# A hybrid encoder block: y in tiles of token halves, and two units' first products ahead of the second half's sums

## The chip, the cores and the metric

One core of a Trainium2 chip runs the whole program in one launch. The number that counts is the device time of one execution in microseconds (us). The engines are named as in the profile: PE is TensorE's matrix multiplication and PEld its weight load, DVE is VectorE, ACT is ScalarE, POOL is GpSimd, SP is SyncE, which only issues DMAs. Each engine runs its own instructions strictly in the order in which the program holds them; semaphores hold an instruction back until what it reads is there and what it overwrites is free.

## What is computed

A bidirectional encoder block over 1024 tokens of width 1024, in float32. Cut to what matters here:

```python
y = sigmoid(ga) * (h_a @ p_a) + sigmoid(gb) * (h_b @ p_b)
x = x + y @ w_o
xn = rmsnorm(x, norm2)
u = xn @ w_up                       # 1024 x 5632
u = conv3_over_tokens(u) + conv_b   # per channel
a, g = split(u, 2)
x = x + (gelu(g) * a) @ w_down
```

Each float32 matrix product is made of three products of halves: an operand is split into a high part h (rounded to the matrix engine's float32 format) and a low part l = value - h, and h*h, h*l and l*h are summed.

## The kernel before

The program is written in a framework that allocates tiles from pools with a fixed number of buffers, and whose scheduler fixes the order of each engine's instructions ahead of time from its own estimates. So the order of the code is a hint, and the order in the program is what the chip follows.

The change lies between two long stretches. Ahead of it is the product with w_o: y has its channels on partitions, in 8 high and 8 low tiles over all 1024 tokens (`yh`, `yl`). `wo_piece(w, cg, b0)` makes 256 columns of two blocks of 128 tokens with 48 matmuls and adds them to the residual `acc` (L956), the x1 tiles. The last two column groups are done for token blocks 0 to 3 first, then `norm0` normalises these blocks, then the column groups are done for blocks 4 to 7.

Behind it is the up projection in the class `Up`. It works in 22 units j of 128 a-columns and 128 g-columns, and each unit uses Strassen's scheme in Winograd's form on 2 by 2 blocks: 7 products instead of 8. The four blocks of the activations are two token halves by two halves of the channels: 11 and 12 are the first token half, 21 and 22 the second. Besides 11, 12 and 22 the products need four sums, S1 to S4, each over both token halves. A block or sum has four k-pieces kk of 128 channels by 512 tokens, each as a high and a low part (`block`, the tiles A.. and AS..). One product is 12 matmuls: 4 pieces, 3 split products. `first(u)` makes products 11 and 12, which need the first token half alone; `rest(u)` makes S2, S1, S3, S4 and 22.

`rows(half)` makes the norm of four token blocks: it stores x1 to DRAM (L1019, on GpSimd's queue), sums squares on ACT (L1021), takes the power -1/2 on GpSimd (L224) and scales the rows (L1024, `nxs`). `turn` transposes four 128 by 128 pieces on PE into one PSUM tile (L1030). `norm0` brings blocks 11 and 12 out of PSUM: the high part on ACT (L1044), a full copy f on DVE (L1045), the low part on GpSimd (L1046). `norm1` does the same for the second half (L1064 to L1067) and makes the sums on DVE (L1072 to L1075); the eight pieces' low parts are shared by DVE and GpSimd (L81).

`prep(u)` makes a unit's weights: four pairs of blocks, the high parts `uh` by ACT casts (L80) and the low parts `ul` by GpSimd (L81), and the weight sums on DVE (L1123 to L1130). The tiles whi and wlo have 4 buffers each, shared by the w_o weights and the units' weights. In `run`, the first unit's weights are loaded and made only when the w_o stage has been left.

Of the kernel before, what the change touches and what calls it, by code (L numbers as in the profile page):

```python
# [877 lines left out]
def merge_ffn(K, ha_d, hb_d, out):  # L878
    nc, tc, I = K.nc, K.tc, K.I
    V, G, A, T = nc.vector, nc.gpsimd, nc.scalar, nc.tensor  # L880
    with tc.tile_pool(name="mf", bufs=1, reuse_waits="tile") as fp, ExitStack() as es:
# [25 lines left out]
        for gidx, (hx, pname) in enumerate(((K.ha, "p_a"), (hb, "p_b"))):  # L907
            if gidx == 1:
                while len(hb[0]) < KT:
                    load_hb()  # L910
                y = h2("y", "A")
            for cg in range(4):
# [3 lines left out]
                for cb in range(2):  # L916
# [5 lines left out]
                    for half in range(2):  # L922
                        t = slice(half * 512, half * 512 + 512)
                        ps = K.small()
                        K.proj_cm(ps, w, cb * P, hx, half)
                        if gidx == 0:
                            if len(hb[0]) < KT:
                                load_hb()
                            V.scalar_tensor_tensor(ya[m][:, t], tg[:, t], 1.0, ps, op0=ALU.add, op1=ALU.mult)
                        else:  # L930
                            V.scalar_tensor_tensor(tg[:, t], tg[:, t], 1.0, ps, op0=ALU.add, op1=ALU.mult)
                            V.tensor_tensor(tg[:, t], tg[:, t], ya[m][:, t], op=ALU.add)
                            K.split(y[0][m][:, t], y[1][m][:, t], tg[:, t])
# [16 lines left out]
        def wo_piece(w, cg, b0):  # L950
            ps = K.small()
            for j in range(2):
                K.proj_tm(ps[:, j * 256:(j + 1) * 256], w, y, b0 + j)
# [12 lines left out]
        up = Up(K, g4, acc, g2, fp)  # L966
        for i in range(2):
# [12 lines left out]
class Up:  # L980
# [31 lines left out]
    def rows(self, half, scr):  # L1012
# [3 lines left out]
        for b4 in range(4):  # L1016
            blk = half * 4 + b4
            x, o = self.acc[blk], scr[b4]
            nc.gpsimd.dma_start(self.x1_d[blk * P:(blk + 1) * P, :], x)  # L1019
# [4 lines left out]
            nc.vector.tensor_scalar(o, x, r, None, op0=ALU.mult)  # L1024
# [7 lines left out]
    def norm0(self, scr, psf):  # L1032
# [16 lines left out]
    def norm1(self):  # L1049
        K, nc, G, V = self.K, self.K.nc, self.K.nc.gpsimd, self.K.nc.vector  # L1050
        xs = self.rows(1, [self.g4("nxs") for _ in range(4)])
        f2s = []

        def turns(kk):
            f2 = self.g4("f2", tag="wk")
            f2s.append(f2)
            for i in range(2):
                k = kk + 4 * i
                ps = K.small()
                self.turn(xs, k, ps)  # L1060
                t = slice(i * 512, i * 512 + 512)
                if i == 1:
                    self.b22 = self.block("22", kk, "A" if kk < 2 else "B")
                    nc.scalar.activation(self.b22[0], ps, AF.Copy, scale=self.g2[:, k:k + 1])  # L1064
                V.tensor_scalar(f2[:, t], ps, self.g2[:, k:k + 1], None, op0=ALU.mult)
                if i == 1:
                    V.tensor_tensor(self.b22[1], f2[:, t], self.b22[0].bitcast(F32), op=ALU.subtract)  # L1067

        def sums(kk):
            f, f2 = self.f[kk], f2s[kk]  # L1070
            a11, a12, a21, a22 = f[:, :512], f[:, 512:], f2[:, :512], f2[:, 512:]
            V.tensor_tensor(a22, a21, a22, op=ALU.add)  # L1072
            V.tensor_tensor(a21, a11, a21, op=ALU.subtract)
            V.tensor_tensor(a11, a22, a11, op=ALU.subtract)
            V.tensor_tensor(a12, a12, a11, op=ALU.subtract)  # L1075
            for n, (name, v) in enumerate((("S2", a11), ("S1", a22), ("S3", a21), ("S4", a12))):
                h, l = self.block(name, kk, "B" if kk >= 2 and n == 0 else "A")
                K.split(h, l, v, G if n % 2 else V)

        turns(0)  # L1080
        sums(0)
        turns(1)
        sums(1)
        turns(2)
        turns(3)
        sums(2)
        sums(3)

# [18 lines left out]
    def prep(self, u):  # L1107

        K, V, G = self.K, self.K.nc.vector, self.K.nc.gpsimd

        def pair(*blocks):
            h = K.wp.tile([P, 1024], F32R, tag="whi", bufs=NH, name=K.nm("uh"))
            l = K.wp.tile([P, 1024], F32R, tag="wlo", bufs=NW, name=K.nm("ul"))
            for n, v in enumerate(blocks):
                t = slice(n * 512, n * 512 + 512)
                K.split(h[:, t].rearrange("p (k c) -> p k c", k=4), l[:, t].rearrange("p (k c) -> p k c", k=4), v, G)
# [3 lines left out]
        yield  # L1120
# [4 lines left out]
        V.tensor_tensor(t2, u["b22"], u["b12"], op=ALU.subtract)  # L1125
        pair(t2, u["b12"])
# [16 lines left out]
    def first(self, u):  # L1143
# [4 lines left out]
        u["s"] = self.g4("s", tag="wk")  # L1148
        u["ua"], u["ug"] = self.g4("u", tag="acc"), self.g4("u", tag="acc")
        A.copy(u["s"][:, :512], u["X"])  # L1150
        self.product(u, 1, Y, True, True)
        V.tensor_tensor(u["ua"][:, :512], Y, u["s"][:, :512], op=ALU.add)

    def rest(self, u, nxt):
# [4 lines left out]
        A.copy(u["s"][:, 512:], X)  # L1159
        self.product(u, 3, Z, True, True)  # L1160
        z = self.g4("z", tag="wk")
# [5 lines left out]
        V.tensor_tensor(u["ug"][:, :512], Z, u["s"][:, 512:], op=ALU.add)  # L1167
# [20 lines left out]

    def run(self):
        us, ps = [self.load(0), self.load(1)], []  # L1190
        ps = [self.prep(u) for u in us]
        next(ps[0])
        self.first(us[0])
        self.norm1()
        next(ps[0]), next(ps[0]), next(ps[0])
        for j in range(NFF):
            u = us[j]
            if j:
                self.first(u)
            if j + 1 < NFF:  # L1200
# [112 lines left out]
```

## Time and profile before

| | us |
|---|---|
| median of 3 runs | 2235.78 (2235.41 to 2236.54) |
| the profiled execution | 2236.34 |
| its span, first to last instruction | 2234.6 |
| PE busy in it | 2136.8 (96%) |
| mean granted PE clock | 0.986 of full speed |

The span is 1.7 us shorter than the execution's own time, which also holds what lies around the first and the last instruction. PE is busy for 96% of the span, but that is an average: the stage of this change is only some 75 us long, and there PE is busy for three quarters of the time. A stretch can be read by windows (busy time of each engine between two moments), by waits (who waited for whom) and by the timeline of one engine.

### The profile page before, as it was taken

The page shows a single profiled execution, that of the slowest core. Times are in us where ns is not written, and L with a number is a line of the kernel's source. Part 1 is how long each engine was busy: PE and PEld are TensorE (multiplying, and loading weights), DVE is VectorE, ACT ScalarE, POOL GpSimd, SP SyncE. Part 2 cuts the span into 40 slices and gives each one's busy share as a digit, 9 for nine tenths or more (in the row PEclk, how much of TensorE's full clock was granted, in tenths as well). Part 3 has the DMA queues.
Part 4 walks back from the last instruction along what each step waited for, and adds up shares of the span by engine and source line. Part 5 has one row for each costly group of instructions (what it writes and reads, how often), then busy time and mean ns, then how long its engine had stood idle before and what let it go on. Part 6 is the DMA issues. An engine that isn't in the chain of part 4 may idle for free.

```text
span 2234.6 us, 30400 instructions
## 1 busy us (share of the span) xinstructions
PE 2136.8 (96%) x11936; PEld 1834.9 (82%) x11936; DVE 1303.3 (58%) x1986; ACT 912.0 (41%) x1659; POOL 680.5 (30%) x529
## 2 busy tenths in 40 slices
PE   7999999989999899999999999996999999999999
PEld 6778878888899789889888878995777877788887
DVE  4455253446597787878956334338677667673422
ACT  4333132235456556556545122124544544452221
POOL 0131101143252442533500010026666666640000
PEclk9999999999999999999999999997999999999999
DMA  3123212132211222112223574222222222295501
GB/s 124 38 82 104 66 57 76 53 71 60 57 34 50 58 40 47 57 38 62 56 90 117 160 170 147 71 86 66 76 76 85 76 68 83 85 346 193 176 29 38
DMA packets 185168, 193.85 MB, mean 87 GB/s; under 512 B 38616, under 2 KB 153336, under 8 KB 185024
## 3 DMA queue, kind: packets, MB, share of 16 engines
q1 hardware_dynamic: 175296, 156.96, 24.5%
q0 software_dynamic: 9728, 34.94, 4.4%
q8 instruction: 94, 1.54, 0.3%
q14 instruction: 50, 0.41, 0.1%
HBM read 144.38 MB, written 39.09 MB: 82 GB/s over the span
## 4 chain that ended last, share of the span: by engine, by line
PE 70%; DVE 13%; DMA 6%; issue 4%; ACT 4%; POOL 2%; SPq 0%; DVEq 0%; ACTq 0%; POOLq 0%
PE sm L105 11%; PE sm L106 11%; PE sm L107 11%; PE pj L105 8%; PE pj L106 7%; PE pj L107 7%; DMA wraw<-in_w_in_dram 3%; PE big L681 3%; PE pt L713 2%; DVE smx L685 2%; DVE p L693 1%; PE cr L465 1%; PE cr L470 1%; PE cr L467 1%; PE po L106 1%
## 5 line engine op out<-in xcount | busy, mean ns | idle before, releaser
L107 PE MATMUL pj<-whi,xn 128*128 128x256 f32 x960 | 274.1, 286 | 0.0
L105 PE MATMUL pj<-whi,xn 128*128 128x256 f32 x960 | 273.3, 285 | 0.2
L106 PE MATMUL pj<-wlo,xn 128*128 128x256 f32 x960 | 273.4, 285 | 0.0
L105 PE MATMUL pj<-xn,whi 128*128 128x512 f32 x512 | 211.9, 416 | 6.0 <-ACT xn L246 3.3
L106 PE MATMUL pj<-xn,whi 128*128 128x512 f32 x512 | 208.4, 407 | 0.0
L107 PE MATMUL pj<-xn,wlo 128*128 128x512 f32 x512 | 208.3, 407 | 0.0
L687 ACT ACTIVATE p<-big,smx 128x1024 f32<-128x1024 f32 x128 | 143.0, 1119 | 123.8 <-DVE smx L685 87.2
L81 POOL TENSOR_TENSOR ul<-ur,uh 128x512 fp32r<-128x512 f32 x110 | 173.3, 1592 | 38.4 <-ACT uh L80 38.4
L105 PEld LDWEIGHTS pj<-whi,xn 128*128 128x128 f32 x960 | 181.9, 189 | 3.2 <-ACT kT L300 0.3
L106 PEld LDWEIGHTS pj<-wlo,xn 128*128 128x128 f32 x960 | 181.8, 189 | 1.9
L107 PEld LDWEIGHTS pj<-whi,xn 128*128 128x128 f32 x960 | 181.7, 189 | 1.0
L80 ACT CAST whi<-wraw 128x1024 fp32r<-128x1024 f32 x88 | 92.2, 1048 | 216.5 <-DMA wraw<-in_w_in_dram 103.1
L685 DVE TENSOR_REDUCE smx<-big 128x1 f32<-128x1024 f32 x128 | 154.5, 1218 | 36.8 <-PE big L681 36.0
L81 DVE TENSOR_TENSOR wlo<-wraw,whi 128x1024 fp32r<-128x1024 f32 x54 | 67.6, 1251 | 168.3 <-ACT whi L80 168.3
L105 PE MATMUL sm<-AS,uh 128*128 128x512 f32 x352 | 140.5, 401 | 15.9 <-ACT AS L80 11.0
L681 PE MATMUL big<-kst,qst 128*128 128x512 f32 x512 | 146.6, 406 | 4.8 <-DMA kst<-kst 4.8
L106 PE MATMUL sm<-AS,uh 128*128 128x512 f32 x352 | 141.3, 401 | 0.6 <-POOL AS L81 0.6
L107 PE MATMUL sm<-AS,ul 128*128 128x512 f32 x352 | 140.7, 401 | 0.0
L106 PE MATMUL sm<-dl,hh 128*128 128x512 f32 x352 | 139.5, 396 | 0.0
L105 PE MATMUL sm<-dh,hh 128*128 128x512 f32 x352 | 139.0, 396 | 0.0
L107 PE MATMUL sm<-dh,hl 128*128 128x512 f32 x352 | 138.9, 396 | 0.0
L224 POOL TENSOR_TENSOR inv<-inv,mhalf 128x2 f32<-128x2 f32 x32 | 23.0, 718 | 366.9 <-DVE inv L223 308.5
(289 smaller groups left out, 5450.7 us busy)
## 6 DMA issues: line engine op xcount, KB each, us to landing
ur<-in_w_up_dram SPq DMA_DIRECT2D x88, 256.0 KB, 3.4
wr<-in_w_down_dram SPq DMA_DIRECT2D x44, 512.0 KB, 5.6
wraw<-in_w_in_dram SPq DMA_DIRECT2D x40, 512.0 KB, 5.5
wraw<-in_w_in_dram SPq DMA_DIRECT2D x48, 256.0 KB, 4.6
h_d<-cv POOLq DMA_DIRECT2D x22, 512.0 KB, 3.0
hr<-h_d SPq DMA_DIRECT2D x22, 512.0 KB, 6.5
x<-in_x_dram SPq DMA_DIRECT2D x16, 512.0 KB, 4.9
sig<-tg SPq DMA_DIRECT2D x32, 256.0 KB, 2.1
```

The costliest lines, as they stand in the source:

```text
L80: self.nc.scalar.copy(hi, src)
L81: (lo_eng or self.nc.vector).tensor_tensor(lo, src, hi.bitcast(F32), op=ALU.subtract)
L105: mm(ps, a[0], b[0], start=start, stop=False, skip_group_check=again)
L106: mm(ps, a[0], b[1], start=False, stop=False, skip_group_check=again)
L107: mm(ps, a[1], b[0], start=False, stop=stop, skip_group_check=again)
L224: K.nc.gpsimd.tensor_tensor(out, scr, K.mhalf[:scr.shape[0], :width], op=ALU.pow)
L465: T.matmul(nps[:, :MV + 1], pm[:, t], va[:, j, :], start=True, stop=i == 0)
L467: T.matmul(nps[:, :MV + 1], qs[:, t], C, start=False, stop=True)
L681: T.matmul(sps[c_][:, half * 512:half * 512 + 512], o.q[st.qp][:, c_, t], o.k[half][:, c_, s_, :], start=s_ == 0, stop=s_ == 1)
L685: V.tensor_reduce(sm[:, c_:c_ + 1], sp, op=ALU.max, axis=AX.X, negate=True)
L687: K.mark = A.activation(p_, sp, AF.Exp, bias=sm[:, c_:c_ + 1], accum_out=sm[:, 2 + c_:3 + c_]).ins
L713: T.transpose(pt[:, kk * 256 + j * P:kk * 256 + (j + 1) * P], st.w[j][:, kb * P:(kb + 1) * P], K.ident)
```

## The change

The y tiles become [token half][pair of k], so that the first half's tiles are free when the first half's w_o products are done; the blocks 11 and 12 go into them, and the copies f into the x1 buffers of the first half. The loads of units 0 and 1 are issued before the last w_o products, and `ahead()` makes the first pair of both units' weights there. `run` is now: the second half's `rows`, `first` of unit 0, all transposes (`norm1b`), `first` of unit 1, and then the sums (`norm1c`), ordered by name instead of by piece. The x1 stores move from GpSimd's queue to SP's. GpSimd no longer makes low parts of blocks and sums, nor those of unit 0's weights; DVE does these straight from PSUM where it can, and the f copies go to ACT.

```diff
-                y = h2("y", "A")
+                yt = [[[g4("y", F32R) for _ in range(KT // 2)] for _ in range(2)] for _ in range(2)]
+                y = [[[yt[p][half][k // 2][:, k % 2 * 512:k % 2 * 512 + 512] for half in range(2)]
+                      for k in range(KT)] for p in range(2)]
...
         up = Up(K, g4, acc, g2, fp)
+        up.us = [up.load(0), up.load(1)]
...
             for bp in range(2):
                 wo_piece(ws[i], 2 + i, 4 + bp * 2)
+        up.ahead()
         es.close()
...
-            nc.gpsimd.dma_start(self.x1_d[blk * P:(blk + 1) * P, :], x)
+            nc.sync.dma_start(self.x1_d[blk * P:(blk + 1) * P, :], x)
...
-            nc.vector.tensor_scalar(o, x, r, None, op0=ALU.mult)
+            if half == 1 and b4 % 2 == 0:
+                nc.scalar.activation(o, x, AF.Copy, scale=r)
+            else:
+                nc.vector.tensor_scalar(o, x, r, None, op0=ALU.mult)
...
-            f = self.g4("f", tag="B")
+            f = self.g4("f", tag="acc")
...
-                h, l = self.block(name, kk, "B")
+                h, l = self.block(name, kk, "A")
-                nc.scalar.activation(h, ps, AF.Copy, scale=self.g2[:, k:k + 1])
-                V.tensor_scalar(f[:, t], ps, self.g2[:, k:k + 1], None, op0=ALU.mult)
-                G.tensor_tensor(l, f[:, t], h.bitcast(F32), op=ALU.subtract)
+                nc.scalar.activation(h, ps, AF.Copy, scale=gk)
+                V.scalar_tensor_tensor(l, ps, gk, h.bitcast(F32), op0=ALU.mult, op1=ALU.subtract)
+                nc.scalar.activation(f[:, t], ps, AF.Copy, scale=gk)
...
+    def norm1b(self):
+        for kk in range(4):
...
+            self.turn(self.xs1, kk, ps)
+            nc.scalar.activation(v, ps, AF.Copy, scale=self.g2[:, kk:kk + 1])
...
+            self.turn(self.xs1, kk + 4, ps)
+            self.p22.append(ps)
+    def norm1c(self):
...
+            V.scalar_tensor_tensor(v, self.p22[kk], gk, a21, op0=ALU.mult, op1=ALU.add)
+            V.tensor_tensor(a21, f[:, :512], a21, op=ALU.subtract)
+            V.tensor_tensor(f[:, :512], v, f[:, :512], op=ALU.subtract)
+            K.split(*self.block("S2", kk, "A"), f[:, :512])
+            S1.append(v)
+        for kk in range(4):
+            K.split(*self.block("S1", kk, "A"), S1[kk])
+        for kk in range(4):
+            gk = self.g2[:, 4 + kk:5 + kk]
+            h, l = self.block("22", kk, "B")
+            nc.scalar.activation(h, self.p22[kk], AF.Copy, scale=gk)
+            V.scalar_tensor_tensor(l, self.p22[kk], gk, h.bitcast(F32), op0=ALU.mult, op1=ALU.subtract)
+        for kk in range(4):
+            K.split(*self.block("S3", kk, "B"), self.f2[kk])
+        for kk in range(4):
+            f = self.f[kk]
+            V.tensor_tensor(f[:, 512:], f[:, 512:], f[:, :512], op=ALU.subtract)
+            K.split(*self.block("S4", kk, "B"), f[:, 512:])
...
+        lo = V if early else G
...
+    def ahead(self):
+        self.ps = [self.prep(u, True) for u in self.us[:1]] + [self.prep(self.us[1])]
+        for p in self.ps:
+            next(p)
...
-        next(ps[0])
-        self.first(us[0])
-        self.norm1()
+        us, ps = self.us, self.ps
+        self.norm1a()
+        s = self.g4("s", tag="B")
+        self.first(us[0], s[:, :512])
+        self.norm1b()
+        self.first(us[1], s[:, 512:])
+        self.norm1c()
```

What this makes of the order of instructions shows at three places. On PE, first, where the second half's transposes end; before the change, sums come next (AS tiles, `sm` are PSUM tiles, `uh` and `ul` unit 0's weights):

```order
L1030 MATMUL sm_14430<-ident,nxs_14310 128x128
L1030 MATMUL sm_14430<-ident,nxs_14311 128x128
L1030 MATMUL sm_14430<-ident,nxs_14312 128x128
L1030 MATMUL sm_14430<-ident,nxs_14313 128x128
L105 MATMUL sm_14279<-AS_2116_14363,uh_14474 128x512
L105 MATMUL sm_14503<-AS_2118_14367,uh_14474 128x512
L106 MATMUL sm_14279<-AS_2117_14364,uh_14474 128x512
```

The same place on PE in the changed kernel, where the transposes (L1039 there) are followed by product 11 of unit 1:

```order
L1039 MATMUL sm_14393<-ident,nxs_14289 128x128
L1039 MATMUL sm_14393<-ident,nxs_14290 128x128
L1039 MATMUL sm_14393<-ident,nxs_14291 128x128
L1039 MATMUL sm_14393<-ident,nxs_14292 128x128
L105 MATMUL sm_14398<-A_2073_13999,uh_14279 128x512
L106 MATMUL sm_14398<-A_2074_14000,uh_14279 128x512
L107 MATMUL sm_14398<-A_2073_13999,ul_14280 128x512
```

So 24 matmuls that need nothing of the second half have moved between the transposes and the first sum. On DVE, second, where the second half's sums begin; before (f are full copies, A block 22's low part, AS low parts of sums):

```order
L1065 TENSOR_SCALAR f_2111_14342<-sm_14343,g_13279 128x512
L1125 TENSOR_TENSOR ut_14531<-ur_14270,ur_14267 128x512
L1065 TENSOR_SCALAR f_2111_14342<-sm_14349,g_13279 128x512
L1067 TENSOR_TENSOR A_2115_14355<-f_2111_14342,A_2114_14354 128x512
L1072 TENSOR_TENSOR f_2111_14342<-f_2111_14342 128x512
L1130 TENSOR_TENSOR ur_14270<-ur_14270,ut_14531 128x4x128
L1073 TENSOR_TENSOR f_2111_14342<-f_13981,f_2111_14342 128x512
L1074 TENSOR_TENSOR f_13981<-f_2111_14342,f_13981 128x512
L1075 TENSOR_TENSOR f_13981<-f_13981 128x512
L81 TENSOR_TENSOR AS_2117_14364<-f_13981,AS_2116_14363 128x512
```

The same place on DVE in the changed kernel (S is sum S1, f_2114 and f_2119 hold block 21):

```order
L1087 SCALAR_TENSOR_TENSOR S_2128_14428<-sm_14359,g_13279,f_2114_14352 128x512
L1088 TENSOR_TENSOR f_2114_14352<-f_13993,f_2114_14352 128x512
L1087 SCALAR_TENSOR_TENSOR S_2128_14428<-sm_14370,g_13279,f_2114_14352 128x512
L1089 TENSOR_TENSOR f_13993<-S_2128_14428,f_13993 128x512
L1087 SCALAR_TENSOR_TENSOR S_2131_14441<-sm_14382,g_13279,f_2119_14375 128x512
L1088 TENSOR_TENSOR f_2114_14352<-f_14013,f_2114_14352 128x512
L1098 SCALAR_TENSOR_TENSOR A_2139_14467<-sm_14359,g_13279,A_2138_14466 128x512
L1103 TENSOR_TENSOR f_13993<-f_13993 128x512
```

The sums of the four pieces are now made first and the low parts follow, and no preparation of weights stands between them. On GpSimd, third, from the second half's last two powers on; before:

```order
L224 TENSOR_TENSOR nr_14338<-nss_14336,mhalf 128x1
L81 TENSOR_TENSOR ul_14475<-ur_14261,uh_14474 128x512
L81 TENSOR_TENSOR ul_14475<-ut_14470,uh_14474 128x512
L81 TENSOR_TENSOR ul_14481<-ut_14470,uh_14480 128x512
L81 TENSOR_TENSOR ul_14481<-ur_14264,uh_14480 128x512
L81 TENSOR_TENSOR ul_14488<-ur_14264,uh_14487 128x512
L81 TENSOR_TENSOR ul_14492<-ur_14267,uh_14491 128x512
L81 TENSOR_TENSOR ul_14492<-ur_14270,uh_14491 128x512
L81 TENSOR_TENSOR AS_2119_14368<-f_2111_14342,AS_2118_14367 128x512
L81 TENSOR_TENSOR AS_2123_14376<-f_13981,AS_2122_14375 128x512
```

GpSimd in the changed kernel at the same place (ul_14562 and on are unit 1's low parts, ul_14618 unit 2's):

```order
L224 TENSOR_TENSOR nr_14317<-nss_14315,mhalf 128x1
L81 TENSOR_TENSOR ul_14562<-ut_14557,uh_14561 128x512
L81 TENSOR_TENSOR ul_14562<-ur_13751,uh_14561 128x512
L81 TENSOR_TENSOR ul_14594<-ut_14557,uh_14593 128x512
L81 TENSOR_TENSOR ul_14594<-ur_13754,uh_14593 128x512
L81 TENSOR_TENSOR ul_14614<-ur_13754,uh_14613 128x512
L81 TENSOR_TENSOR ul_14618<-ur_14523,uh_14617 128x512
```

Only unit 1's weights are left on GpSimd while the sums are made.

## Rows read from the trace of the kernel before

**Rows 1.** The page, part 1: busy us (share of the span) xinstructions
```profile
PE 2136.8 (96%) x11936; PEld 1834.9 (82%) x11936; DVE 1303.3 (58%) x1986; ACT 912.0 (41%) x1659; POOL 680.5 (30%) x529
```
**Rows 2.** Windows: us, busy us (instructions) of each engine, clock, DMA
```profile
1412.00:1507.90 95.90, 95.86 (x806) 95.39 (x804) 29.12 (x58) 17.15 (x26) 16.46 (x19) 1.00 0.23 78
1507.90:1582.35 74.45, 56.02 (x212) 41.86 (x213) 61.48 (x68) 34.77 (x57) 46.54 (x34) 0.84 0.21 64
```
**Rows 3.** Waits of PE, 1507.8 to 1582.4: us, times, longest us
```profile
PE sm L105 <- ACT AS L80: 11.0, 4, 5.0
PE sm L1030 <- DVE u L1152: 2.5, 1, 2.5
PE sm L105 <- ACT uh L80: 2.3, 1, 2.3
```
**Rows 4.** Timeline of PE: start us, us, line, tile, count
```profile
1507.26 0.60 PE L1030 MATMUL big<-ident,nxs 128*128 128x128 f32 x4
...
1512.63 0.63 PE L105 MATMUL sm<-A,uh 128*128 128x512 f32 x1
...
1516.89 0.63 PE L106 MATMUL sm<-A,uh 128*128 128x512 f32 x1
1517.32 1.99 PE L1030 MATMUL sm<-ident,nxs 128*128 128x128 f32 x14
...
1577.21 0.40 PE L107 MATMUL sm<-A,ul 128*128 128x512 f32 x1
...
1582.35 0.39 PE L105 MATMUL sm<-AS,uh 128*128 128x512 f32 x1
```
**Rows 5.** Timeline of DVE, the same stretch
```profile
1507.46 0.76 DVE L956 SCALAR_TENSOR_TENSOR x<-sm,x 128x256 f32<-128x256 f32 x2 [0.21 <-PE sm L107]
...
1525.11 0.74 DVE L1065 TENSOR_SCALAR f<-sm,g 128x512 f32<-128x512 f32 x1
...
1538.35 1.82 DVE L1074 TENSOR_TENSOR f<-f,f 128x512 f32<-128x512 f32 x1
...
1549.01 0.68 DVE L81 TENSOR_TENSOR AS<-f,AS 128x512 fp32r<-128x512 f32 x1
1549.61 0.68 DVE L1075 TENSOR_TENSOR f<-f 128x512 f32<-128x512 f32 x1
...
1557.35 0.68 DVE L81 TENSOR_TENSOR AS<-f,AS 128x512 fp32r<-128x512 f32 x1
```
**Rows 6.** Timeline of GpSimd, the same stretch
```profile
1506.63 1.25 POOL L224 TENSOR_TENSOR nr<-nss,mhalf 128x1 f32<-128x1 f32 x2
...
1538.32 1.30 POOL L81 TENSOR_TENSOR AS<-f,AS 128x512 fp32r<-128x512 f32 x1 [2.60 <-ACT AS L80]
...
1559.61 1.30 POOL L81 TENSOR_TENSOR ul<-ut,uh 128x512 fp32r<-128x512 f32 x1 [0.17 <-ACT uh L80]
```
**Rows 7.** Timeline of ACT, the same stretch
```profile
1489.13 1.27 ACT L1044 ACTIVATE A<-big,g 128x512 fp32r<-128x512 f32 x2 [4.77 <-PE big L1030]
...
1508.48 1.05 ACT L1021 ACTIVATE nxs<-x 128x1024 f32<-128x1024 f32 x1
...
1531.55 2.18 ACT L80 CAST AS<-f 128x512 fp32r<-128x512 f32 x4 [3.62 <-DVE f L1074]
...
1565.80 1.24 ACT L1176 ACTIVATE cv<-u,cb,cw 128x1024 f32<-128x1024 f32 x1
```
**Rows 8.** Instructions of line 247: duration ns min/median/max, first and last start
```profile
L247 DVE SCALAR_TENSOR_TENSOR xn<-cr,g,xn x16: 741/745/752, 18.2 to 50.2; 128x512 fp32r<-128x512 f32 x16
```
**Rows 9.** Timelines of GpSimd, DVE and PE in a later unit
```profile
1785.10 5.03 POOL L81 TENSOR_TENSOR ul<-ur,uh 128x512 fp32r<-128x512 f32 x4
...
1785.17 5.51 DVE L1123 TENSOR_TENSOR ut<-ur,ur 128x512 f32<-128x512 f32 x1 [3.60 <-POOL ul L81]
...
1796.74 0.51 PE L105 MATMUL sm<-AS,uh 128*128 128x512 f32 x1 [3.12 <-ACT s L1159]
```
**Rows 10.** Transfers issued by line 1019 (the x1 stores): us to landing
```profile
DMA to landing us min/median/max: 3.0/4.4/6.4
```

More of the change, by code (lines that the diff above doesn't have):

```diff
@@ L952, in wo_piece @@
             for j in range(2):
-                K.proj_tm(ps[:, j * 256:(j + 1) * 256], w, y, b0 + j)
+                half, b = divmod(b0 + j, 4)
+                K.proj_tm(ps[:, j * 256:(j + 1) * 256], w, [[t_[half] for t_ in p_] for p_ in y], b)
             for j in range(2):
@@ L1047, in norm0 @@
+                V.scalar_tensor_tensor(l, ps, gk, h.bitcast(F32), op0=ALU.mult, op1=ALU.subtract)
+                nc.scalar.activation(f[:, t], ps, AF.Copy, scale=gk)
             self.f.append(f)
[L1049 to L1087, printed above, removed]
@@ new lines, in norm1a @@
+    def norm1a(self):
+        self.xs1 = self.rows(1, [self.g4("nxs", tag="B") for _ in range(4)])
+    def norm1b(self):
+        K, nc = self.K, self.K.nc
+        self.f2, self.p22 = [], []
+        for kk in range(4):
+            if kk % 2 == 0:
+                f2 = self.g4("f2", tag="wk")
+            ps = K.small()
+            self.turn(self.xs1, kk, ps)
+            v = f2[:, kk % 2 * 512:kk % 2 * 512 + 512]
+            nc.scalar.activation(v, ps, AF.Copy, scale=self.g2[:, kk:kk + 1])
+            self.f2.append(v)
+            ps = K.small()
+            self.turn(self.xs1, kk + 4, ps)
+            self.p22.append(ps)
@@ new lines, in norm1c @@
+    def norm1c(self):
+        K, nc, V = self.K, self.K.nc, self.K.nc.vector
+        S1 = []
+        for kk in range(4):
+            if kk % 2 == 0:
+                s1 = self.g4("S1", tag="B")
+            f, a21 = self.f[kk], self.f2[kk]
+            v = s1[:, kk % 2 * 512:kk % 2 * 512 + 512]
+            gk = self.g2[:, 4 + kk:5 + kk]
[7 more added lines that the diff above has]
+        for kk in range(4):
+            gk = self.g2[:, 4 + kk:5 + kk]
+            h, l = self.block("22", kk, "B")
[3 more added lines that the diff above has]
+            K.split(*self.block("S3", kk, "B"), self.f2[kk])
+        for kk in range(4):
+            f = self.f[kk]
+            V.tensor_tensor(f[:, 512:], f[:, 512:], f[:, :512], op=ALU.subtract)
+            K.split(*self.block("S4", kk, "B"), f[:, 512:])
@@ L1105, in load, with prep @@
         return u
-    def prep(self, u):
+    def prep(self, u, early=False):
         K, V, G = self.K, self.K.nc.vector, self.K.nc.gpsimd
+        lo = V if early else G
         def pair(*blocks):
@@ L1115, in pair @@
                 t = slice(n * 512, n * 512 + 512)
-                K.split(h[:, t].rearrange("p (k c) -> p k c", k=4), l[:, t].rearrange("p (k c) -> p k c", k=4), v, G)
+                K.split(h[:, t].rearrange("p (k c) -> p k c", k=4), l[:, t].rearrange("p (k c) -> p k c", k=4), v, lo)
             u["w"].append((h, l))
         pair(u["b11"], u["b21"])
-        yield
+        if not early:
+            yield
         t = K.wp.tile([P, 1024], F32, tag="wraw", bufs=NR, name=K.nm("ut"))
@@ L1125, in prep @@
         V.tensor_tensor(t2, u["b22"], u["b12"], op=ALU.subtract)
+        if early:
+            yield
         pair(t2, u["b12"])
@@ L1147, in first @@
         self.product(u, 0, u["X"], True, True)
-        u["s"] = self.g4("s", tag="wk")
+        if s is None:
+            u["s"] = self.g4("s", tag="wk")
+            s = u["s"][:, :512]
         u["ua"], u["ug"] = self.g4("u", tag="acc"), self.g4("u", tag="acc")
-        A.copy(u["s"][:, :512], u["X"])
+        A.copy(s, u["X"])
         self.product(u, 1, Y, True, True)
-        V.tensor_tensor(u["ua"][:, :512], Y, u["s"][:, :512], op=ALU.add)
+        V.tensor_tensor(u["ua"][:, :512], Y, s, op=ALU.add)
     def rest(self, u, nxt):
@@ L1158, in rest @@
         self.product(u, 2, X, False, True)
-        A.copy(u["s"][:, 512:], X)
+        z = self.g4("z", tag="wk")
+        s2 = u["s"][:, 512:] if "s" in u else z[:, 512:]
+        A.copy(s2, X)
         self.product(u, 3, Z, True, True)
-        z = self.g4("z", tag="wk")
         A.copy(z[:, :512], Z)
@@ L1166, in rest @@
         self.product(u, 5, Z, False, True)
-        V.tensor_tensor(u["ug"][:, :512], Z, u["s"][:, 512:], op=ALU.add)
+        V.tensor_tensor(u["ug"][:, :512], Z, s2, op=ALU.add)
         step()
```

11 lines of the change are left out of this document (5 added, 6 removed).

## The prediction

> **What bounds the kernel now.** The page comes first: PE is busy for 96% of the span, DVE for 58% [rows 1], so a gain can only come from a stage in which PE waits. The windows show where the change lies in this. In the w_o stage PE is busy for 95.86 of 95.90 us; from its last transposes to the middle of unit 2 it is busy for 56.02 of 74.45 us, at a mean granted clock of 0.84 [rows 2]. The waits of that stretch name whom PE waits for: 11.0 us for the casts of the sums, 2.5 for transposes held by DVE, 2.3 for the first unit's weights [rows 3].
>
> How much is lost there? The stretch begins when the last four transposes of `norm0` end, at 1507.9, and I end it at 1582.35, where unit 2's products 11 and 12 are done [rows 4]. Its PE work is the same before and after, 180 matmuls and 32 transposes. At full clock a matmul of 512 columns takes 0.234 us (22 steps from 1577.21 to 1582.35 [rows 4]); at the lower level of 1.2 GHz, after PE had waited, 0.426 (10 steps from 1512.63 to 1516.89 [rows 4]). A transpose takes 0.14 (14 in 1.99 us [rows 4]). So the work needs 42.0 + 4.5 = 46.5 us of the 74.45: **28.0 us are lost**, 18.4 as waits (74.45 - 56.02) and the rest at the lower clock. That is all that this change can win; behind it PE's order is the same until the last unit.
>
> Behind the waits for the casts stands DVE. From the first L1065 at 1525.1 to the last low part's end at 1558.0 [rows 5] it runs 38 instructions, 0.87 us each. Two of them back to back take 0.60 (1549.01 to 1549.61 [rows 5]); one that meets GpSimd takes 1.82 instead of about 0.7 (L1074 at 1538.35, beside GpSimd's low part from 1538.32 [rows 5, 6]).
>
> **The change part by part.** I go along PE's order after the change, from the same start at 1507.9.
>
> *Ahead of it.* The y tiles hold the same numbers and cost the same splits. The early loads are issued while w_o runs; x1's stores land 3.0 to 6.4 us after their issue [rows 10], and the first f that takes an x1 buffer comes behind the first high parts, two w_o pieces (11.4 us) after that buffer's last sum: both are hidden. ACT gets eight more copies (two take 1.27 [rows 7]) and four casts of weights in the last 14 us of w_o. Before PE can transpose the third and fourth k-pairs, the PSUM tiles of the first two must be emptied: four casts (2.18 [rows 7]), the high parts and copies (0.6 each) and DVE's queue of low parts come to 5.7 us after the whi tiles come free, an estimate, and PE has 43 w_o matmuls of 0.119 us (806 instructions in 95.9 us [rows 2]) and 8 transposes there, 6.2 us. I take 0; if GpSimd's two low parts there (1.3 each [rows 6]) hold DVE longer, 2 us.
>
> *First products of unit 0.* The weights are made, so the wait of 2.3 and its low part's go, and PE stays at full clock: 24 x 0.234 = 5.6 us, to 1513.5.
>
> *Transposes.* They now need all four blocks. The last w_o result is added by 1508.2 [rows 5]; ACT is busy with casts and copies until about 1510.2, then squares two blocks (1.05 each [rows 7]), GpSimd takes the powers (0.6 each [rows 6]), and ACT scales (as long as a square, 1.05): with 0.7 for handing over, an estimate, 1514.7. PE waits **1.2 us**. Then 32 transposes, 4.5 us, to 1519.2.
>
> *First products of unit 1.* 5.6 us, to 1524.8. They cover the first sums; this is where 24 matmuls stood behind sums before.
>
> *Sums.* DVE can begin at the second transposed tile, about 1516.6. Until the last low part of S2 its order has 35 instructions. Nine read PSUM; no row here has this form in this stage, the nearest is 0.745 [rows 8], and I take 0.67 to 0.745. The others take 0.60 to 0.72. At 0.68 the 35 end at 1540.4. GpSimd keeps two low parts of unit 1 back to back in this time, 2 x 1.3 us [rows 6]. One later row shows what that can do: a DVE sum of 0.68 us took 5.51 while GpSimd ran four low parts, 5.03 us, and got in only behind the last [rows 9]. So I add the whole 2.6 us: 1543.0. The Trainium skill (SBUF — State Buffer, section "SBUF: two separate sides") says that the two engines hold the shared port pair for one whole instruction and the other blocks; by it DVE would wait behind one low part and the sum would be 1.3 us smaller. The row of 5.51 does not agree with that, and I go by the row. PE, at the lower clock after its waits, is some matmuls behind (4 for the last piece, up to 12 more): S2 and S1 of both units are done at **1545**. Between 1524.8 and there PE does 48 matmuls, 11.2 us, so it loses 9.0. Bounds: 1541, when all DVE instructions take 0.60 and meet nothing; 1550, when they average 0.87 as before and PE runs its backlog at 0.426.
>
> *Behind the sums.* Unit 0's X must be copied out before S3, and ACT has that of unit 1 behind a cast that waits for a weight tile: **0.9 us**. Then S4, S3 of both and 22 of unit 0 are 60 matmuls. Unit 2's first weights need the whi tile that 22 of unit 0 reads last: a cast (0.6) and a GpSimd low part (1.3) behind it, less three matmuls: **1.5 us**. Both units' convolutions come late together (ACT 1.24 each [rows 7]), and the copy of unit 2's X stands behind them: **1.0 us**, between 0 and 4.
>
> *The sum.* Lost after: 1.2 + 9.0 + 0.9 + 1.5 + 1.0 = 13.6 us, where 28.0 were lost before. The profiled execution took 2236.3, so 2236.3 - 14.4 = 2221.9. It is 0.6 us above the median of the runs shown, 2235.8; by the median the sum is 2221.4. I say **2222**. At the end of the up stage the order moves a little, but no wait of PE stood there that I cost.
>
> **Rivals.**
>
> *The sums stay the bound.* For it: 37 DVE instructions make the second half after, 38 before, and the stall of 5.51 shows that few meetings suffice. Against it: eight low parts of GpSimd and two sets of weight sums are gone from between them. At 0.87 each, S2's last low part comes at 1516.6 + 30.5 = 1547.1, and PE ends S1 at about 1551: 6 us of the gain go, **2228**.
>
> *No change.* The 14.4 us are spent whole: to the loss of the case above, 4 us of late convolutions and 4 us at the lower clock over the first products of unit 1 would be added. **2236**, and nothing in the rows makes all of it likely.
>
> *The sums are quick.* S1 and S2 end at 1541 and the three small waits are covered: 1.2 + 5.0 lost, **2214**.
>
> *Slower, by the w_o stage.* PE has no idle time there now [rows 2], so every wait put into it counts in full. The transposes of the third and fourth k-pairs wait for PSUM tiles that ACT now empties with twice the copies, in a row with casts that wait for w_o's own weight tiles. I found 5.7 us of work against 6.2 of cover. It decides from 14.4 us of such waits on; if ACT's and DVE's chain took three times as long, 17 us against 6.2 in two places, that is 22 us, **2243**. Against it: ACT is busy for 17 of 96 us there [rows 2], and the three durations in the chain are rows of this case.
>
> **How the numbers follow.** The forecast 0.64; sums the bound 0.14; quick 0.09; no change 0.07; slower 0.06. What a measurement can tell from no change is 0.2%, 4.5 us. The first three are faster by more than that but for a small part of the second: faster 0.86, same 0.08, slower 0.06. The range holds the bounds of the sums and the small waits and reaches to the case of 2228 and to that of 2214: 2213 to 2231, with some 0.85 inside.
>
> **What would show it.** Right: PE goes on at 1508 without a wait and at full clock into unit 0's product 11; the transposes follow within 2 us; the only long waits of PE are for casts or low parts of S2 and S1, between 1525 and 1545, about 9 us; unit 2's first low part costs 1 to 2 us; the same stretch of 180 matmuls and 32 transposes takes about 60 us. Wrong: waits of PE on PSUM tiles inside w_o; DVE sums of over 1.6 us in a row in that time, without GpSimd beside them; PE at the lower clock until S4; or waits in later units that were not there.

## The result, and the profile after

The changed kernel takes 2221.0 us, median of 4 runs, where the kernel before took 2236.2 beside it: ratio 0.9931, 95% interval 0.9919 to 0.9944. The forecast was 2222. The profiled execution took 2222.2 us, its span 2220.2, 14.4 us less than before. Two executions in the experiments, 7281 us with y's tiles alone and 2902 us with the squares behind, lie far outside all others and are left out of the ratios.

The page, part 1, as in [rows 1], and two windows, as in [rows 2]: the w_o stage, and the stretch from its last transposes to the end of unit 2's products 11 and 12 (columns: us, busy us and instructions of PE, PEld, DVE, ACT, POOL, clock, DMA share, GB/s).

```profile
PE 2132.0 (96%) x11936; PEld 1832.6 (83%) x11936; DVE 1293.1 (58%) x1991; ACT 921.5 (42%) x1673; POOL 638.9 (29%) x498
...
1412.00:1508.15 96.15, 96.15 (x808) 95.81 (x807) 34.17 (x64) 24.87 (x38) 6.32 (x8) 1.00 0.25 82
1508.15:1566.53 58.38, 50.59 (x216) 39.58 (x215) 44.96 (x65) 35.65 (x59) 17.03 (x13) 0.91 0.20 63
```

PE is still busy all through the w_o stage. The stretch that took 74.45 us takes 58.4. GpSimd was busy for 46.5 us in it and is now for 17.

The waits of PE between 1400 and 1600 us (us in total, times, longest), as in [rows 3]:

```profile
PE sm L105 <- ACT AS L80: 3.6, 1, 3.6
PE sm L105 <- ACT f L1056: 2.0, 1, 2.0
PE sm L106 <- DVE AS L81: 1.4, 1, 1.4
PE sm L107 <- POOL ul L81: 0.7, 1, 0.7
PE sm L105 <- ACT s L1185: 0.3, 1, 0.3
```

The casts of the sums cost 3.6 us instead of 11.0. The second line was not foreseen. The timeline of PE shows each at its place, as in [rows 4]:

```profile
1507.80 0.60 PE L1039 MATMUL big<-ident,nxs 128*128 128x128 f32 x4
1508.15 0.48 PE L105 MATMUL sm<-A,uh 128*128 128x512 f32 x1
...
1513.24 0.79 PE L105 MATMUL sm<-A,uh 128*128 128x512 f32 x1 [2.05 <-ACT f L1056]
1513.83 0.63 PE L106 MATMUL sm<-A,uh 128*128 128x512 f32 x1
1514.26 0.63 PE L107 MATMUL sm<-A,ul 128*128 128x512 f32 x1
...
1517.64 3.66 PE L1039 MATMUL sm<-ident,nxs 128*128 128x128 f32 x32
1521.05 0.48 PE L105 MATMUL sm<-A,uh 128*128 128x512 f32 x1
...
1526.74 0.39 PE L105 MATMUL sm<-AS,uh 128*128 128x512 f32 x1
...
1528.80 0.50 PE L107 MATMUL sm<-AS,ul 128*128 128x512 f32 x1 [0.67 <-POOL ul L81]
...
1533.40 1.05 PE L105 MATMUL sm<-AS,uh 128*128 128x512 f32 x2 [3.63 <-ACT AS L80]
1535.89 0.80 PE L106 MATMUL sm<-AS,uh 128*128 128x512 f32 x1 [1.45 <-DVE AS L81]
...
1546.93 0.39 PE L105 MATMUL sm<-AS,uh 128*128 128x512 f32 x1
...
1566.53 0.39 PE L105 MATMUL sm<-AS,uh 128*128 128x512 f32 x1
```

PE runs from the last transposes into unit 0's product 11 without a wait. Then product 12 waits 2.05 us, and seven matmuls behind it go at the lower clock (start to start 0.43 instead of 0.234; the granted clock is 0.50 of full speed from 1513.24 to 1516.39, in the window below). Unit 1's first products end at 1526.7, S2 and S1 of both units at 1546.9. From there to 1566.53 PE does 84 matmuls in 19.6 us, 0.233 each: nothing is lost there.

What product 12 waits for is the last line of this timeline of ACT:

```profile
1510.42 1.07 ACT L1027 ACTIVATE nxs<-x 128x1024 f32<-128x1024 f32 x1
...
1511.46 1.06 ACT L1027 ACTIVATE nxs<-x 128x1024 f32<-128x1024 f32 x1
...
1512.50 0.69 ACT L1056 ACTIVATE f<-big,g 128x512 f32<-128x512 f32 x1
```

f is not an input of product 12. The copy of f reads `norm0`'s last PSUM tile. That product 12's result goes where this tile was is read from the kernel, which gives up the PSUM tiles of `norm0` and makes eight new ones between the two; the trace shows that the copy ends at 1513.19 and the product starts at 1513.24. The copy stands behind two squares of the second half. The clock behind the wait, in a window as above:

```profile
1513.24:1516.39 3.15, 3.15 (x7) 2.48 (x8) 1.98 (x3) 1.62 (x2) 1.04 (x2) 0.50 0.00 0
```

In the sums, DVE meets GpSimd once; rows of DVE and of GpSimd in the same time:

```profile
1528.05 2.92 DVE L81 TENSOR_TENSOR AS<-f,AS 128x512 fp32r<-128x512 f32 x2
...
1534.56 1.28 DVE L81 TENSOR_TENSOR AS<-f,AS 128x512 fp32r<-128x512 f32 x2
...
1541.78 1.89 DVE L81 TENSOR_TENSOR AS<-f,AS 128x512 fp32r<-128x512 f32 x3
...
1527.46 1.29 POOL L81 TENSOR_TENSOR ul<-ut,uh 128x512 fp32r<-128x512 f32 x1 [13.18 <-ACT uh L80]
1528.70 1.73 POOL L81 TENSOR_TENSOR ul<-ur,uh 128x512 fp32r<-128x512 f32 x1
```

Two of DVE's instructions take 2.92 us there and 1.28 elsewhere in the sums (1534.56), so the meeting costs 1.64. In the later units the waits are those of before, shifted: the one of 3.12 us in [rows 9] comes 15.2 us earlier. One short wait is new, where the up stage ends:

```profile
1781.50 0.50 PE L105 MATMUL sm<-AS,uh 128*128 128x512 f32 x1 [3.12 <-ACT s L1185]
...
1966.46 0.50 PE L105 MATMUL sm<-AS,uh 128*128 128x512 f32 x1 [0.54 <-ACT z L1187]
```

### The profile page after: what moved, and what is told of

The parts are those of the page before. It is cut to its first block, busy times and chain, and to the rows that moved or that the text cites. A ratio compares the mean times of both kernels' runs of the same rounds, so it can differ in the third digit from the quotient of the medians.

```text
span 2220.2 us, 30362 instructions
## 1 busy us (share of the span) xinstructions
PE 2132.0 (96%) x11936; PEld 1832.6 (83%) x11936; DVE 1293.1 (58%) x1991; ACT 921.5 (42%) x1673; POOL 638.9 (29%) x498
## 4 chain that ended last, share of the span: by engine, by line
PE 68%; DVE 13%; DMA 6%; issue 5%; ACT 4%; POOL 2%; SPq 0%; ACTq 0%; DVEq 0%; POOLq 0%
PE sm L105 11%; PE sm L106 11%; PE sm L107 11%; PE pj L105 8%; PE pj L106 7%; PE pj L107 7%; PE big L681 3%; DMA wraw<-in_w_in_dram 3%; PE pt L713 2%; DVE smx L685 2%; DVE p L693 1%; PE cr L465 1%; PE cr L470 1%; PE cr L467 1%; PE po L106 1%
## 5 line engine op out<-in xcount | busy, mean ns | idle before, releaser
L81 POOL TENSOR_TENSOR ul<-ur,uh 128x512 fp32r<-128x512 f32 x105 | 165.2, 1590 | 41.8 <-ACT uh L80 41.8
```

Of the source, the lines that this page charges most:

```text
L81: (lo_eng or self.nc.vector).tensor_tensor(lo, src, hi.bitcast(F32), op=ALU.subtract)
```

## The experiments

The part of the program ahead of this stage ends at another time in each profile (product 11 of unit 0 starts between 1501.6 and 1509.8 us in kernels whose work up to there hardly differs), so the totals carry some us of chance. The table therefore has, beside the ratio, times counted in the timeline of PE from the end of w_o's last instruction, where product 11 could start: to the start of the 128th instruction (in most kernels the last of 24 + 24 matmuls of first products, 32 transposes and 48 matmuls of S2 and S1) and to the start of the 260th. At full speed the 260 need 56.6 us: 228 matmuls of 0.233, and 32 transposes of 0.107 (1517.64 to 1521.05 above).

| kernel | ratio to before (95%) | to the 128th | to the 260th |
|---|---|---|---|
| changed, the profile above | 0.9931 (0.9919 to 0.9944) | 38.5 | 69.3 |
| changed, again | 0.9925 (0.9911 to 0.9938) | 37.0 | 67.8 |
| before with y's tiles alone | 0.9997 (0.9987 to 1.0006) | | |
| casts moved in the code | 0.9921 (0.9907 to 0.9936) | 36.9 | 67.7 |
| loads late | 0.9995 (0.9986 to 1.0004) | 49.8 | 80.7 |
| loads late, stores on GpSimd | 1.0020 (1.0010 to 1.0030) | 53.7 | 84.5 |
| stores on GpSimd | 0.9926 (0.9914 to 0.9939) | 37.1 | 67.9 |
| unit 1 behind | 0.9960 (0.9945 to 0.9974) | 43.5 | 74.3 |
| low parts on GpSimd | 0.9945 (0.9929 to 0.9962) | 38.8 | 70.2 |
| squares behind | 0.9933 (0.9917 to 0.9950) | 37.6 | 68.4 |
| sums first | 0.9902 (0.9883 to 0.9921) | 28.5 | 60.2 |
| sums first, again | 0.9904 (0.9889 to 0.9919) | 28.5 | 60.2 |
| sums first, casts behind | 0.9909 (0.9894 to 0.9923) | 31.2 | 62.9 |

The 1.5 us between the first two rows are seven matmuls at the lower clock behind product 12's wait, in the one profile and not in the other, though the wait is there in both (2.05 and 2.01 us). The other kernels are compared with 67.8. Not every part of the change was taken out by itself: no run has the copies of f back on VectorE, all rows scaled by VectorE, or the change without the split tiles of y.

**y's tiles alone.** The kernel before, with the diff's lines on `y` and `wo_piece` and nothing else of it.

> The kernel before, with only the tiles of y split into token halves. Theory (the w_o stage waited for nothing at y, so the finer tiles alone change nothing, and the gain lies behind the w_o stage): 2236 us, within 1 us of the kernel before. Rival (the finer tiles let the w_o pieces of the first half, and so the norm, start earlier, and a part of the 15 us comes from them): 2232 us or less.

2234.0 us beside 2234.0. The tiles alone are worth nothing. Whether the rest could do without them, this run doesn't show.

**When the first weights are made.** Three kernels. In the first only the call moves:

```diff
-        up.ahead()
         es.close()
...
         self.norm1a()
+        self.ahead()
```

> The changed kernel, with the casts of the first two units' weights issued behind the second half's norm (the loads stay early); TensorE's order of instructions is the same. Theory (the early weights hide the wait for casts that stood between the last transposes of the first half and unit 0's products): product 11 of unit 0 waits for its high and low weights behind the four squares, so TensorE waits 3 to 5 us there, the transposes of the second half start at about 1521 to 1522 instead of 1517.6, and the run takes 2224 to 2227 us. Rival (what bounds is the sums on VectorE, which start when the scaled rows and the transposes are there): the wait shows, but is made up in the wait for the sums, and the run takes 2221 to 2222 us.

2218.5 us, and no wait for weights: the order on ACT around this stage is the same as in the changed kernel. A likely reason is that the scheduler places the casts by when their data is there, and the loads stayed early. So this run tells only that the place of the call decides nothing. The second moves the loads as well:

```diff
-        up.us = [up.load(0), up.load(1)]
...
-        up.ahead()
...
         self.norm1a()
+        us = self.us = [self.load(0), self.load(1)]
+        self.ahead()
```

> The changed kernel, with the loads of the first two units' weights, and so their casts, back behind the w_o stage (in run, behind the second half's squares); the casts stand behind the squares and scaled copies on ScalarE, as they did in the kernel before. The run in which only the casts moved in the code kept them early, since their data was there. Theory (the early weights are worth something): product 11 of unit 0 waits for the casts some 8 us after the last transposes of the first half, the transposes of the second half are done about 3 to 7 us later than in the changed kernel, and the sums with them: the 260 matmuls and transposes from product 11 on take 71 to 75 us instead of 68 to 69.3, ratio to before 0.9945 to 0.9965. Rival (the wait for the rows of the second half covers it, and the sums set the end): within 1.5 us, ratio 0.992 to 0.994.

2233.1 us beside 2234.4: the whole gain is gone, more than the theory gave. Product 11 waits 7.0 us for the casts, and the 260 take 80.7 us. (The 78.7 of the next expectation counts 19 matmuls of w_o in, which stand behind the last transposes in this kernel.) The third also puts the stores back (`nc.gpsimd.dma_start` for the x1 stores), to see whether the queue does it:

> The run with the loads late lost the whole gain; there the loads came behind the eight stores of x1 on SP's queue, the last of which was issued at 1508 us, and the first cast waited 2.6 us for data. Here the loads stay late, and the stores go back to GpSimd's queue, as both were in the kernel before. Theory A (the loss came from the queue: the loads had to pass the stores): the casts find their data, the wait ahead of product 11 falls from 7.0 to 2 to 3.5 us, the 260 matmuls and transposes from product 11 on take 69 to 73 us instead of 78.7, ratio to before 0.993 to 0.9955. Theory B (it came from the casts and low parts of eight blocks falling into the sums, whatever the queue): 75 to 79 us, ratio 0.9965 to 1.

2239.5 us beside 2234.8: slower than before. Counted as in the expectation, from the last transposes on, the 260 take 82.3 us; that and the ratio of 1.002 lie above theory B's ranges too. Its waits from 1503 to 1560 us:

```profile
PE sm L105 <- ACT AS L80: 6.5, 2, 5.4
PE sm L107 <- POOL ul L81: 6.4, 1, 6.4
PE sm L105 <- ACT uh L80: 4.0, 2, 3.4
...
```

The wait ahead of product 11 falls to 3.4 us, as theory A has it, but that is not where the gain goes. DVE's sums run from 1517.11 to 1547.64, 30.5 us, where they take 24.6 in the kernel with only the casts moved, whose weights stayed early (1514.80 to 1539.36): ten instructions for the weights of units 0 and 1 stand among them, 10 x 0.60 us. And a low part of unit 1 on GpSimd, for which PE then waits 6.4 us, takes 12.36 us beside them. Rows of GpSimd, then of DVE, then the first and last of DVE's sums in the kernel with the casts moved:

```profile
1536.40 12.36 POOL L81 TENSOR_TENSOR ul<-ur,uh 128x512 fp32r<-128x512 f32 x1 [16.80 <-ACT uh L80]
...
1517.11 0.75 DVE L1085 SCALAR_TENSOR_TENSOR S<-sm,g,f 128x512 f32<-128x512 f32 x1 [2.35 <-ACT f L1070]
...
1536.73 1.88 DVE L81 TENSOR_TENSOR AS<-f,AS 128x512 fp32r<-128x512 f32 x3
...
1546.36 1.28 DVE L81 TENSOR_TENSOR AS<-f,AS 128x512 fp32r<-128x512 f32 x2
...
1514.80 0.75 DVE L1086 SCALAR_TENSOR_TENSOR S<-sm,g,f 128x512 f32<-128x512 f32 x1
...
1537.47 1.89 DVE L81 TENSOR_TENSOR AS<-f,AS 128x512 fp32r<-128x512 f32 x3
```

Of the two, theory B names the cause, though the loss is larger than it gave: what the early weights buy is more than the 2.3 us of [rows 3]. In these two runs a part of the loss is the wait ahead of product 11 (7.0 and 3.4 us), and the rest goes with work for the weights that now lies in DVE's chain, and beside it on GpSimd, instead of ahead of the sums.

**The stores alone.**

```diff
-            nc.sync.dma_start(self.x1_d[blk * P:(blk + 1) * P, :], x)
+            nc.gpsimd.dma_start(self.x1_d[blk * P:(blk + 1) * P, :], x)
```

> The changed kernel, with only the stores of x1 back on GpSimd's queue. Theory (with the weights loaded early, nothing on SP's queue waits behind the stores, and no wait near the w_o stage names them): the 260 matmuls and transposes from product 11 on take 68 to 69.4 us, as in the changed kernel, ratio to before 0.992 to 0.9945. Rival (GpSimd holds up the scale factors of the rows, whose powers it computes, while it issues the stores): 0.5 to 3 us more.

2218.1 us beside 2217.8 for the changed kernel, and 67.9 against 67.8 us. The queue of the stores is worth nothing here.

**Unit 1's first products behind unit 0's S1.**

```diff
+        if then:
+            with K.tc.issue_after(K.lastmm):
+                self.first(then, self.s1)
...
-        self.first(us[1], s[:, 512:])
```

> The changed kernel, with unit 1's first two products (24 matmuls, 5.6 us) held behind unit 0's S1 product instead of ahead of the sums. Theory (they fill 5.6 us of the time in which TensorE would wait for the sums): the wait for the sums starts at about 1521 instead of 1526.7, the S2 and S1 parts are there at about the same time as before (1542), and of the work that then remains TensorE has some 36 matmuls (8.4 us) instead of 19 (4.5 us): 3.9 us lost, range 3 to 6, 2225 us. Rival (the order of the products doesn't matter, since the sums end at the same time and S3 and S4 would make TensorE wait otherwise): within 1 us, 2221 to 2222.

2226.1 us, 6.5 us more than the changed kernel to the 260th instruction, above the theory's range. PE reaches the sums 5.6 us early and waits through them (waits from 1503 to 1560 us):

```profile
PE sm L106 <- DVE AS L81: 5.3, 3, 3.4
PE sm L105 <- ACT AS L80: 4.5, 2, 2.8
```

The waits in the sums are 9.8 us instead of 5.6 (3.6, 1.3 and 0.7), 4.2 more, as the theory has it. The other 2.3 go into the clock: it is at 0.89 of full speed over the 260 instructions, against 0.95 in the changed kernel. The theory left that out.

**Eight low parts on GpSimd.** `K.split(..., nc.gpsimd)` for S1 and S4 in `norm1c`.

> The changed kernel, with the eight low parts of S1 and S4 in the second half's sums given to GpSimd again (as before the change), everything else kept. Theory (VectorE and GpSimd hold each other up when both take SBUF operands, as two low parts of weights already did: 1.64 us more on VectorE): GpSimd takes 1.3 us and more for each, S1's low parts end later than VectorE's would, and the span grows by 2 to 6 us (2223 to 2227). Rival (VectorE is the bound of the sums and eight of its instructions of 0.6 us go): the sums end up to 2.4 us earlier, 2218.5 to 2221.

2223.2 us, and 2.4 us more to the 260th. GpSimd, then DVE:

```profile
1531.54 6.79 POOL L81 TENSOR_TENSOR AS<-S,AS 128x512 fp32r<-128x512 f32 x4 [2.40 <-ACT AS L80]
...
1532.07 1.76 DVE L1103 TENSOR_TENSOR f<-f 128x512 f32<-128x512 f32 x1
1533.75 1.76 DVE L81 TENSOR_TENSOR AS<-f,AS 128x512 fp32r<-128x512 f32 x1
```

The two engines take turns: one instruction of each in 1.7 us, and each of DVE's takes 1.1 us more than alone (0.68). Giving eight away saves DVE 4.8 us, and the meetings cost more. Leaving GpSimd out is a gain of its own, 2.4 us in the stretch for these eight. In the total it is 4.7, against 2218.5 us for the kernel with the casts moved, run beside it: behind the stretch PE waits 2.1 us for a copy where it waits 0.3 in the changed kernel.

**The wait of product 12.**

```diff
-            nc.scalar.activation(o, x, AF.Square, accum_out=ss[:, 0:1])
+            if half == 1 and b4 > 1:
+                with K.tc.issue_after(self.lastf):
+                    nc.scalar.activation(o, x, AF.Square, accum_out=ss[:, 0:1])
...
```

> The changed kernel, with the last two squares of the second half's norm held on ScalarE behind the last copy of f, for which product 12 of unit 0 waited 2.05 us. Theory (product 12 waits only for that copy, since its PSUM tile takes the place of the tile that the copy reads; behind it stands the wait for the scaled rows, which the prediction put at 1.2 us): the 2.05 us go, a wait of 1.5 to 2.2 us for the scaled rows appears ahead of the transposes, and these start 7.4 to 7.9 us after product 11's start instead of 8.0 (9.5 in the changed kernel's profile, where the clock was at half for seven matmuls): 0.3 us gained, 1.8 with the clock. Rival (the wait is for something else of ScalarE's, the high part of the last block 12): the wait stays within 0.5 us of 2.05.

The wait falls to 1.40 us, not to nothing: with the squares gone from ahead of it, the copy of f waits for DVE, whose low part of block 12 stands behind four low parts of unit 0's weights. It still ends when the copy does (1514.17 us, and the product starts at 1514.22), so the copy is what it waits for. Behind it the scaled rows come up, as the theory has it, though less of them (rows of PE; two transposes stand ahead of the second row):

```profile
1514.22 0.50 PE L105 MATMUL sm<-A,uh 128*128 128x512 f32 x1 [1.40 <-ACT f L1060]
...
1517.87 3.51 PE L1043 MATMUL sm<-ident,nxs 128*128 128x128 f32 x30 [0.36 <-ACT nxs L1035]
```

Thirty of the 32 transposes start 8.1 us after product 11's start, all 32 at 8.0 in the changed kernel: nothing is gained, and the theory's 0.3 us were not there.

**S2 and S1 first.**

```diff
+            cv = V.tensor_tensor(l, S1[kk], h.bitcast(F32), op=ALU.subtract).ins
+        with K.tc.issue_after(cv), K.tc.issue_after(ca):
+            for kk in range(4):
+                K.split(*self.block("S3", kk, "B"), self.f2[kk])
...
```

(S4 and block 22 stand in the same `with`; `ca` is ScalarE's copy beside `cv`.)

> The changed kernel, with the splits of S3 and S4 and the copies of block 22 held behind S1's low parts on VectorE and ScalarE, so that VectorE makes S2 and S1 first. Theory (what is left of the stall is the order of VectorE's chain: S2 and S1, for which TensorE waits, share it with S3, S4 and block 22, which are needed 11 us later): S1's last low part ends some 14 us after the transposes' first results instead of 25, and the wait in the sums falls from 9.1 us to 1 to 3: 6 us gained on the changed kernel (4 to 8), ratio to before 0.989 to 0.9915. Rival (S3, S4 and block 22 are then late instead, and the wait only moves): the sum of the waits stays within 1.5 us, ratio 0.992 to 0.994.

2210.8 us beside 2234.4. The stall in the sums is gone. This was run again beside the changed kernel:

> The changed kernel as it is, on the same chip and beside the kernel with the sums first, for a direct comparison. Theory: ratio to before 0.9915 to 0.9945; the 260 matmuls and transposes from product 11 on take 67.9 us, or 69.3 where the clock falls behind product 12's wait.

> The kernel with the sums of S2 and S1 first, unchanged, with more rounds and beside the changed kernel. Theory (it gains 8.4 us on the changed kernel, by the stretch of its trace): ratio to before 0.988 to 0.9915, 5 to 11 us under the changed kernel of this call. Rival (the earlier start of its stretch was chance, and part of the gain is given back behind it): 2 to 5 us under it.

2211.0 against 2217.8 us, 6.7 less, and 7.6 less in the stretch: by the total within the theory and above its rival, whose idea that a part is given back is right as well, by the wait of 1.6 us shown last below. Windows of the changed kernel (again), the 260 instructions and the 48 matmuls of S2 and S1:

```profile
1504.53:1572.30 67.77, 60.15 (x263) 47.35 (x262) 55.89 (x71) 40.23 (x65) 26.34 (x18) 0.95 0.21 63
1521.36:1541.50 20.14, 14.53 (x50) 10.28 (x49) 17.16 (x26) 8.69 (x16) 2.96 (x2) 0.83 0.28 79
```

The same two of the kernel with the sums first, and its waits from 1400 to 1600 us:

```profile
1503.55:1563.75 60.20, 57.59 (x262) 45.76 (x261) 54.06 (x71) 39.93 (x65) 26.77 (x17) 1.00 0.23 71
1520.40:1532.04 11.64, 11.46 (x50) 8.86 (x48) 11.64 (x18) 10.03 (x19) 3.38 (x2) 1.00 0.49 135
...
PE sm L105 <- ACT f L1056: 2.0, 1, 2.0
PE sm L105 <- ACT s L1188: 1.6, 1, 1.6
PE sm L107 <- POOL ul L81: 0.6, 2, 0.4
```

48 matmuls take 11.6 us instead of 20.1, at full clock, and the wait for casts is not there any more. DVE's work is the same (54.1 us busy, 55.9 before); only its order is another. One wait of 1.6 us for a copy of X comes in behind the stretch, where the changed kernel waits 0.3.

**And unit 0's later casts behind the rows.** As the last, and the four casts of unit 0's S weights and their low parts held behind the second half's scaled rows:

```diff
-        next(ps[0]), next(ps[0]), next(ps[0])
+        with self.K.tc.issue_after(self.lastna), self.K.tc.issue_after(self.lastnv):
+            next(ps[0]), next(ps[0]), next(ps[0])
```

> The kernel with the sums of S2 and S1 first, and besides the four casts of unit 0's S2, S1, S3 and S4 weights on ScalarE (0.52 us each) held behind the last scaled copy of the second half's rows. Theory (the four casts stand on the way to the copy of f and to the squares): the wait of 2.05 us ahead of product 12 goes, the transposes start 5.4 to 6 us after product 11's start instead of 8.0, and the sums with them: 2 us less than with the sums first alone (1 to 2.7). Rival (VectorE's low parts of these weights come into the sums instead, 2.4 us, and take it back): within 0.7 us of the kernel with the sums first alone.

2.7 us more to the 260th than the kernel with the sums first. The transposes start a little earlier, but the last eight wait for DVE (rows of PE):

```profile
1514.79 2.78 PE L1039 MATMUL sm<-ident,nxs 128*128 128x128 f32 x24
1519.35 1.09 PE L1039 MATMUL sm<-ident,nxs 128*128 128x128 f32 x8 [1.77 <-DVE u L1179]
```

The addition that empties product 12's PSUM tile now stands behind the four low parts. The theory fails; the rival's low parts come in, at another place than it named.

## Why the prediction was right, and where its terms were off

The mechanism was right in each of its three large steps. *The y tiles cost and win nothing by themselves*: shown, both alone and in the w_o stage, where PE is busy for 96.15 of 96.15 us, so the rival that ends slower there is out. *Unit 1's first products cover sums*: shown, 6.5 us when they are put behind. *The loss in the sums falls to 9.0 us*: from 1526.74 to 1546.93 are 20.2 us for 11.2 us of matmuls, 9.0 lost. The stretch was to take about 60 us and took 58.4. Of the signs that the prediction named for being right, two did not come: PE had a long wait outside the sums (2.05 us at product 12), and unit 2's first low part cost nothing.

The terms against the trace. The work now needs 42.0 + 3.4 us, since 32 transposes in a row take 0.107 each and not 0.14; 58.4 - 45.4 = 13.0 us are lost, where the sum had 13.6. (Before, the same work leaves 29.1 us lost and not 28.0, so the stretch gained 16.1.) Its parts:

- *Transposes, 1.2 us.* Measured 4.0 lost from 1508.15 to 1526.74 (18.6 us for 14.6 of work). The scaled rows are done at 1515.1, 0.4 later than I had, but nothing waits for them. The 2.05 us wait is at product 12, for the PSUM tile that the copy of f empties, and most of the rest is the lower clock behind it. The step "PE stays at full clock, to 1513.5" failed: I followed product 12's operands and not the place of its result.
- *Sums, 9.0 us.* The size holds because errors cancel, which is luck. DVE began 2.5 us later than the 1516.6 that I had (1519.1, behind the late transposes), and its S2 ended at 1542.4, not 1543.0: its 35 instructions came every 0.62 us on average, without the meeting, where I took 0.68, and the meeting with GpSimd cost 1.64 us, not 2.6. PE was then 19 matmuls behind, 4.5 us, where I had 2.0. It did not wait for that last low part: its last wait ended at 1535.89, and from there it ran through. Of the 9.0 us, 5.75 are the three waits, and the other 3.3 are mostly the lower clock behind them. Of the rule of the Trainium skill that I set against the row of 5.51 us (SBUF — State Buffer, section "SBUF: two separate sides": the pair of ports is held for one whole instruction), the 1.64 us are nearer to its 1.3 than to my 2.6. The turns in the run with eight low parts on GpSimd agree with it too (1.1 us more for each of DVE's). The 12.36 us of GpSimd's low part do not: by it GpSimd would wait for one instruction of DVE, and 18 of DVE's started while it ran.
- *Behind the sums, 0.9 + 1.5 + 1.0 us.* Nothing of this is in the stretch; the first weights of unit 2 and the copies for unit 0 were in time. Of the last term 0.3 us show just behind it, the wait for the copy of unit 2's X at 1579.

So in the stretch the last three terms were too large by 3.4 us and the first one too small by 2.8. The end of the stretch came 15.8 us earlier than before and the span got 14.4 shorter. The difference was lost at two places, by the starts of the same instructions of PE in both traces: 0.6 us at the copy of unit 2's X, and 0.9 around 1966 us, where PE now waits 0.54 us for a copy (the row further above) at the end of the up stage. The prediction had the first in its last term and put nothing at the second. So it is luck that the span got shorter by exactly the 14.4 us of the sum: the stretch gave more, and what it gave too much was lost behind it.

The step on the early weights gave the right time for a reason too small: I took their worth as the wait of 2.3 us. Two runs show that without the early loads all the rest of the change is worth nothing: product 11 then waits longer (7.0 and 3.4 us), and the weights' work stands in the sums. What was left of the stall, 9.0 us, was not DVE's amount of work, as the bounds of that term took it, but its order: with S2 and S1 first it goes, and that kernel beats both, 2211 us.

## What to carry to other kernels

Where one engine makes operands for another, sort its chain by when each is needed: the same work in another order was worth 7.6 us of the stretch here, and 6.7 of the total, where the whole change had brought 17.1 (2234.8 to 2217.8 us). When products are moved up, look for who empties the PSUM tile that the result goes to, not only for who makes the operands. And early work is worth what it takes out of the chain that is waited for, not the wait that it ends.

## What the runs showed of the hardware that was not expected

VectorE and GpSimd, both on SBUF operands, met in three ways. They took turns, one instruction each in 1.7 us, in the run with eight low parts on GpSimd. VectorE waited 5.51 us through four GpSimd instructions in [rows 9]. And a GpSimd instruction that takes 1.3 us alone took 12.36, ending 1.1 us after VectorE's run of instructions that had lasted from before its start, while these kept their 0.60 us; PE waited 6.4 us for its result. What decides between the three no run here shows.

The 32 transposes in a row, 3.4 us, left the clock where it was: the granted clock is at full speed in them, and behind the first matmul that follows, at 1521.05, they come at 0.23 to 0.24 us from the second on (1521.37).
